# Attention logits of two heads in the two row halves of TensorE, and small float32 matmuls gathered in two banks

## The chip, the cores and the metric

The kernel runs on one core of one Trainium2 chip. The metric is the device time of one launch in microseconds (us), lower is better. TensorE does the matmuls, ScalarE and VectorE read their results out of PSUM and do the elementwise work, GpSimd does masks and reductions over partitions, and all transfers are issued from SyncE.

## The reference

One decoder layer over x of 1024 positions by 1024 channels, everything in float32. The input is normalised and projected once; the columns of the projection feed three branches:

```python
h = rms_norm(x, norm_g)
a_val, a_glu, a_gate, b_q, b_f, b_i, b_gate, c_q, c_k, c_v, c_gate, c_f, merge = split(h @ w_in)
ya = conformer_conv(a_val, a_glu, ...) * silu(a_gate)      # causal depthwise conv of width 31, LayerNorm
yb = hgrn2(b_q, b_f, b_i, ...) * silu(b_gate)              # gated linear recurrence, 8 heads of 128
yc = forgetting_attention(c_q, c_k, c_v, c_f + bias, ...) * silu(c_gate)   # 16 heads of 64
mixed = sum over branches of sigmoid(merge) * (y @ w_branch)
out = x + mixed @ w_out

# forgetting attention, per head, with q and k normalised per head:
logits = q @ k.T / 8 + F[query] - F[key]     # F: cumulative log-sigmoid of c_f
p = softmax(where(key <= query, logits, -inf));  o = p @ v

# recurrence: state = decay * state + k v^T, o = q state; here worked in chunks with levels of 2, 8, 32, 128 steps
```

## The kernel before

**Precision.** A large operand is kept as two float32r parts, high and low (high = rounded copy, low = the rest), and a product is three matmuls: high x high, high x low, low x high. The small matmuls of the recurrence, of the softmax with V, and the transposes are plain float32, which the trace shows as two records a matmul (one for a transpose).

**Staging.** `lin` is the main line: a list of projection jobs, each one weight column block of 128 against 1024 positions, in two halves of 512 and 8 x 3 matmuls each. For each c of 0 to 7 the first part of the list has eight jobs: q, k, v, gate of two attention heads (2c and 2c+1, 64 channels each, so 128 partitions), then q, forget, value, gate of recurrent head c. Everything between those jobs is done in coroutines that issue small matmuls. After that come the conv and merge-gate jobs, the branch projections and the output projection, which this change doesn't touch.

**Order.** `Sched` is a planner that runs while the program is built. It keeps an estimated time for each engine (`use`, `mm`, `act`, ...), and at each point resumes the first coroutine whose ready time has come on TensorE's clock, otherwise the next piece of `lin`. A coroutine that yields a number is ready at that time. The tile framework then orders each engine's instructions by its own timeline and sets the waits.

**Buffers.** Eight PSUM banks of 128 x 512: three rotate among the jobs of `lin`, five (`xbanks`) serve all coroutines through `bget` and `bput`. Work buffers of 1056 columns come from a pool `F` with `NF1` late and `NF2` early slots; job preludes wait until enough are free.

**Attention.** `k_done` (lines 457 to 469) scales k by its norm weight and stores it out of PSUM. For head h the tile `Khi[h]` has k's high part in both 64-row halves, `Klo[h]` the low part in one half and zeros in the other. At its end `qkprep` stores q as `Qst[h]`: high part in one half of the rows, low part in the other. So `Khi[h]` against `Qst[h]` sums high x high and high x low over 128 rows at once, and `Klo[h]` against `Qst[h]` adds low x high. `att` (line 573) walks the blocks of 256 queries from the last to the first, and for each the key blocks j of 128 up to the diagonal; for one j it takes one bank, does two matmuls for each head and evicts the two heads with ScalarE (line 604, adding the forget bias), then yields. Whole blocks have 256 queries; the last key block of each query block has 128. `soft` (line 612) masks, takes the maximum over keys by GpSimd, exponentiates, multiplies with V into `po` (line 655, each head in a 64-column half), and multiplies the folded sum `M` by ones (line 660) into the other half of the same bank.

**Recurrence.** `hgrn` (line 707) works levels of 2, 8 and 32 steps on 32-column quarters of the array, then the chunks of 128: transposes of k (line 831), state products (line 842), the chain of state updates on VectorE (line 852), and outputs (lines 867 and 869). The last four were done by halves of 512 columns with one bank each, and the planner waited `OGY` (3500 ns) or `OGZ` after each half.

Of the kernel before, what the change touches and what calls it, by code (L numbers as in the profile page):

```python
# [8 lines left out]
F32 = mybir.dt.float32  # L9
# [10 lines left out]
P = 128  # L20
# [7 lines left out]
NF2 = 8  # L28
# [171 lines left out]
def build(tc, x, norm_g, w_in, conv_w, conv_b, ln_g, ln_b, hgrn_g, f_bias, qn_g, kn_g,  # L200
# [256 lines left out]
    def k_done(st):  # L457
        def f(half, hs, ps):
            for h in range(2):
                a = slice(h * 64, h * 64 + 64)  # L460
                b = slice(64 - h * 64, 128 - h * 64)
                sc.act(Khi[h][a, hs], ps[a, :], AF.Copy, scale=gk[a])
                sc.act(Khi[h][b, hs], ps[a, :], AF.Copy, scale=gk[a])
                sc.stt(Klo[h][a, hs], ps[a, :], gk[a], Khi[h][a, hs].bitcast(F32),
                       ALU.mult, ALU.subtract)
            sc.act(st["sk"][:, hs], ps, AF.Copy)
            if half == 1:
                sc.start(qkprep(st), f"qk{st['c']}")
        return f

    def qkprep(st):
# [101 lines left out]
    def att(st):  # L573
# [6 lines left out]
        for i in (3, 2, 1, 0):  # L580
# [801 lines left out]
```

## Time and profile before

| what | value |
|---|---|
| median of 3 runs | 1957.88 us (1956.65 to 1960.06) |
| profiled execution | 1957.62 us, span of its instructions 1955.9 us |
| granted TensorE clock, mean of the span | 0.997 |
| busy, TensorE / VectorE / ScalarE / GpSimd | 1908.0 / 1275.5 / 955.5 / 196.4 us |
| DMA, mean | 72 GB/s |

The span runs from the first to the last instruction of the program on the chip; the profiled execution's own time is a little longer. Busy time of TensorE counts a matmul from its start to its modelled end, and successive matmuls overlap, so the start-to-start distance tells what one costs. Names in the rows are the program's tiles: `hT_hi`, `hT_lo` are the normalised input, `whi`, `wlo` a job's weights, `fa` and `fb` work buffers, `gt` an operand of the recurrence, `bank` a PSUM bank. A row says out<-in, then rows x columns of the array in use (128\*128 is all of it, 128\*64 a half, 128\*32 a quarter of its columns) and the moving operand.

### The profile page before, as it was taken

How to read it: one execution, taken by the hardware profiler on the slowest of the kernel's cores; microseconds unless marked ns; L12 is line 12 of the kernel's file. 1: busy time of each engine (PE TensorE's matmuls, PEld its weight loads, DVE VectorE, ACT ScalarE, POOL GpSimd, SP SyncE). 2: the span in 40 equal slices, each digit the busy share in tenths (PEclk: the TensorE clock that was granted, in tenths of full speed). 3: DMA queues.
4: the chain of work that ended last, by engine and by line, in shares of the span. 5: the costliest groups of instructions: out<-in, count | busy, mean ns of one | idle time of the engine just before them, and what ended most of it. 6: DMA issues, size and time to landing. Idle time of an engine off the chain costs nothing.

```text
span 1955.9 us, 27129 instructions
## 1 busy us (share of the span) xinstructions
PE 1908.0 (98%) x11112; PEld 1547.8 (79%) x11112; DVE 1275.5 (65%) x1689; ACT 955.5 (49%) x1524; POOL 196.4 (10%) x157
## 2 busy tenths in 40 slices
PE   5999999999999999999999999999999999999999
PEld 5787877877878778777787878888888888888888
DVE  6358575676664856757557999999996367513431
ACT  5657767757767687677776421111131234312210
POOL 4002120120211201212012100000000110000000
PEclk9999999999999999999999999999999999999999
DMA  4110111111111111111111232222245453212431
GB/s 144 42 44 23 58 40 44 44 34 44 44 45 44 33 44 55 34 44 44 44 44 33 87 108 65 75 70 71 88 160 172 162 175 110 81 54 87 129 120 53
DMA packets 173140, 141.35 MB, mean 72 GB/s; under 512 B 4917, under 2 KB 155445, under 8 KB 173016
## 3 DMA queue, kind: packets, MB, share of 16 engines
q1 hardware_dynamic: 173016, 139.62, 23.3%
q8 instruction: 87, 1.43, 0.3%
q14 instruction: 37, 0.30, 0.1%
HBM read 110.24 MB, written 29.36 MB: 71 GB/s over the span
## 4 chain that ended last, share of the span: by engine, by line
PE 78%; ACT 11%; DVE 5%; issue 3%; DMA 2%; POOL 1%; DVEq 0%; SPq 0%; ACTq 0%; POOLq 0%
PE bank L112 77%; ACT fb L125 5%; ACT L125 3%; DVE fa L129 2%; ACT khi L125 1%; DMA zdram<-fa 1%; ACT fa L125 1%; PE bank L116 1%; DMA fa<-zdram 1%; ACT gt L125 1%; ACT whi L347 1%; DVE wlo L348 1%; DVE fb L129 0%; DVE gt L129 0%; DVE sd L145 0%
## 5 line engine op out<-in xcount | busy, mean ns | idle before, releaser
L112 PE MATMUL bank<-hT_hi,whi 128*128 128x512 f32 x1792 | 709.0, 396 | 7.0 <-ACT fa L125 4.2
L112 PE MATMUL bank<-hT_lo,whi 128*128 128x512 f32 x1792 | 705.7, 394 | 0.0
L112 PE MATMUL bank<-hT_hi,wlo 128*128 128x512 f32 x1792 | 704.3, 393 | 0.9 <-DVE wlo L348 0.9
L112 PEld LDWEIGHTS bank<-hT_hi,whi 128*128 128x128 f32 x1792 | 337.7, 188 | 81.1 <-issue 5.6
L112 PEld LDWEIGHTS bank<-hT_lo,whi 128*128 128x128 f32 x1792 | 337.8, 189 | 72.8 <-issue 8.1
L112 PEld LDWEIGHTS bank<-hT_hi,wlo 128*128 128x128 f32 x1792 | 337.4, 188 | 71.5 <-issue 2.4
L347 ACT ACTIVATE whi<-wraw 128x1024 fp32r<-128x1024 f32 x137 | 145.3, 1060 | 385.0 <-PE bank L112 371.8
L348 DVE TENSOR_TENSOR wlo<-wraw,whi 128x1024 fp32r<-128x1024 f32 x135 | 170.9, 1266 | 201.9 <-ACT whi L347 200.1
L133 DVE SCALAR_TENSOR_TENSOR fa<-fa,taps,fa 128x1024 f32<-128x1024 f32 x240 | 299.8, 1295 | 0.5
L125 ACT ACTIVATE fa<-bank 128x512 f32<-128x512 f32 x191 | 111.3, 594 | 175.6 <-PE bank L112 166.5
L129 DVE TENSOR_TENSOR fa<-fa,fa 128x512 f32<-128x512 f32 (+3 forms) x158 | 131.0, 844 | 71.0 <-ACT fa L125 57.1
L112 PE MATMUL bank<-yhi,whi 128*128 128x512 f32 x384 | 148.7, 389 | 0.9 <-ACT whi L347 0.9
L112 PE MATMUL bank<-ylo,whi 128*128 128x512 f32 x384 | 149.2, 389 | 0.0
L112 PE MATMUL bank<-yhi,wlo 128*128 128x512 f32 x384 | 149.2, 389 | 0.0
L125 ACT ACTIVATE fb<-bank 128x512 f32<-128x512 f32 (+6 forms) x253 | 107.3, 435 | 85.5 <-PE bank L112 46.0
L129 DVE TENSOR_TENSOR fb<-fb,fb 128x256 f32<-128x256 f32 (+3 forms) x158 | 116.8, 754 | 37.8 <-ACT fb L125 22.9
L125 ACT ACTIVATE fb<-bank,negF,rk 128x256 f32<-128x256 f32 x244 | 113.2, 553 | 30.8 <-PE bank L112 22.6
L125 ACT ACTIVATE fb<-fb 128x1024 f32<-128x1024 f32 (+3 forms) x111 | 102.8, 954 | 22.3 <-DVE fb L129 20.9
L125 ACT ACT_TABLE_LOAD x83 | 106.5, 1283 | 8.9 <-DVE fb L129 7.5
L133 DVE SCALAR_TENSOR_TENSOR fa<-fa,bank 128x512 f32<-128x512 f32 x82 | 55.8, 682 | 65.1 <-PE bank L112 64.6
L112 PEld LDWEIGHTS bank<-yhi,whi 128*128 128x128 f32 x384 | 72.1, 188 | 16.2 <-ACT whi L347 1.3
L112 PEld LDWEIGHTS bank<-yhi,wlo 128*128 128x128 f32 x384 | 72.1, 188 | 15.1
(181 smaller groups left out, 2133.9 us busy)
## 6 DMA issues: line engine op xcount, KB each, us to landing
wraw<-in_w_in_dram SPq DMA_DIRECT2D x113, 512.0 KB, 3.8
wraw<-in_w_branch_dram SPq DMA_DIRECT2D x24, 512.0 KB, 3.7
zdram<-fa SPq DMA_DIRECT2D x16, 512.0 KB, 2.6
mdram<-fa SPq DMA_DIRECT2D x32, 256.0 KB, 2.1
fa<-mdram SPq DMA_DIRECT2D x16, 512.0 KB, 3.7
fa<-zdram SPq DMA_DIRECT2D x16, 512.0 KB, 4.4
fa<-in_x_dram SPq DMA_DIRECT2D x9, 512.0 KB, 7.0
yc<-fb SPq DMA_DIRECT2D x8, 512.0 KB, 3.6
```

What stands on the lines that cost most here:

```text
L112: self.nc.tensor.matmul(out, lhsT=lhsT, rhs=rhs, start=start, stop=stop)
L116: self.nc.tensor.transpose(out, in_, ident)
L125: return self.nc.scalar.activation(out, in_, func, **kw)
L129: self.nc.vector.tensor_tensor(out=out, in0=a, in1=b, op=op)
L133: self.nc.vector.scalar_tensor_tensor(out=out, in0=a, scalar=s, in1=b, op0=op0, op1=op1)
L347: pin(nc.scalar.activation(j.hi, j.raw, AF.Copy))
L348: pin(eng.tensor_tensor(out=j.lo, in0=j.raw, in1=j.hi.bitcast(F32), op=ALU.subtract))
```

## The change

q and k of the two heads are stored once, as high part and low part (`Qhi`, `Qlo`, `Khi`, `Klo`), each head in its own 64 partitions; the stacked copies go. The removed lines of the last two parts are left out below; they stand in the listing above. A logit product is now three matmuls a head over 64 rows, head 0 in rows 0 to 63 of the array and head 1 in rows 64 to 127, issued by turns and into two banks, one for each head. One visit does two key blocks. The space of the stacked copies becomes two more early buffers (`NF2` from 8 to 10). In `soft` the matmuls with V are moved behind the folded sum, next to those with ones. In `vprep` and `hgrn` the groups of small float32 matmuls that took one bank after another take two banks at once, with fewer yields.

```diff
--- before.py
+++ after.py
@@ -25,7 +25,7 @@
 NEG = -1e30
 FW = 1056
 NF1 = 10
-NF2 = 8
+NF2 = 10
 RES = 6
 HP = 300
 NLB = 3
@@ -275,12 +275,9 @@
     F.add(f1pool, NF1, "fa", False)
     f2pool = p1ctx.enter_context(tc.tile_pool(name="f2", bufs=1))
     F.add(f2pool, NF2, "fb", True)
-    Qst = [f2pool.tile([P, S], F32R, name=f"qst{h}") for h in range(2)]
-    Khi = [f2pool.tile([P, S], F32R, name=f"khi{h}") for h in range(2)]
-    Klo = [f2pool.tile([P, S], F32R, name=f"klo{h}") for h in range(2)]
+
+    Qhi, Qlo, Khi, Klo = (f2pool.tile([P, S], F32R, name=n) for n in ("qhi", "qlo", "khi", "klo"))
     Gt = [f2pool.tile([P, 4 * KT, 48], F32, name=f"gt{h}") for h in range(2)]
-    nc.vector.memset(Klo[0][64:128].bitcast(F32), 0.0)
-    nc.vector.memset(Klo[1][0:64].bitcast(F32), 0.0)
     ydram = {b: dram.tile([KT, P, S], F32, name=f"y{b}") for b in "bc"}
     zdram = dram.tile([KT, P, S], F32, name="zdram")
     mdram = dram.tile([KT, P, S], F32, name="mdram")
@@ -456,13 +453,8 @@
 
     def k_done(st):
         def f(half, hs, ps):
-            for h in range(2):
-                a = slice(h * 64, h * 64 + 64)
-                b = slice(64 - h * 64, 128 - h * 64)
-                sc.act(Khi[h][a, hs], ps[a, :], AF.Copy, scale=gk[a])
-                sc.act(Khi[h][b, hs], ps[a, :], AF.Copy, scale=gk[a])
-                sc.stt(Klo[h][a, hs], ps[a, :], gk[a], Khi[h][a, hs].bitcast(F32),
-                       ALU.mult, ALU.subtract)
+            sc.act(Khi[:, hs], ps, AF.Copy, scale=gk)
+            sc.stt(Klo[:, hs], ps, gk, Khi[:, hs].bitcast(F32), ALU.mult, ALU.subtract)
             sc.act(st["sk"][:, hs], ps, AF.Copy)
             if half == 1:
                 sc.start(qkprep(st), f"qk{st['c']}")
@@ -517,11 +509,8 @@
         fput(sq, y0)
         yield lambda: not busy["Q"]
         busy["Q"] = True
-        for h in range(2):
-            a = slice(h * 64, h * 64 + 64)
-            b = slice(64 - h * 64, 128 - h * 64)
-            sc.act(Qst[h][a, :], qg[a, sl], AF.Copy)
-            sc.tt(Qst[h][b, :], qg[a, sl], Qst[h][a, :].bitcast(F32), ALU.subtract)
+        sc.act(Qhi, qg[:, sl], AF.Copy)
+        sc.tt(Qlo, qg[:, sl], Qhi.bitcast(F32), ALU.subtract)
         fput(qg)
         st["q"] = st["k"] = True
         st["t"] = sc.cur.last
@@ -542,14 +531,13 @@
     def vprep(st, tag, cb):
         vT, V = st["vT"], st["V"]
         yield
+        pss = yield from bget(2)
+        for k in range(KT):
+            sc.tr(pss[k // 4][:, k % 4 * P:(k % 4 + 1) * P], vT[:, k * P:(k + 1) * P], ident)
         for half in range(2):
-            ps, = yield from bget(1)
-            for q in range(4):
-                k = half * 4 + q
-                sc.tr(ps[:, q * P:(q + 1) * P], vT[:, k * P:(k + 1) * P], ident)
-            sc.act(V[:, half * H2:(half + 1) * H2], ps, AF.Copy)
-            bput(ps)
-            yield
+            sc.act(V[:, half * H2:(half + 1) * H2], pss[half], AF.Copy)
+        bput(*pss)
+        yield
         fput(vT)
         st["v"] = True
         if cb is not None:
@@ -589,21 +577,27 @@
                     d = T[i][:, 0:768].rearrange("p (h t) -> p h t", h=2)
                     v = d[:, :, 0:256] if j == 2 * i else d[:, :, 256:384]
                 blks.append(v)
-            for j in range(2 * i + 2):
-                r = max(0, j - 2 * i)
-                n = 256 - P * r
-                ps, = yield from bget(1)
-                js = slice(j * P, (j + 1) * P)
-                qs = slice(256 * i + P * r, 256 * i + 256)
-                for h in range(2):
-                    o = ps[:, h * 256:h * 256 + n]
-                    sc.mm(o, Khi[h][:, js], Qst[h][:, qs], True, False, n * 0.42 + 6)
-                    sc.mm(o, Klo[h][:, js], Qst[h][:, qs], False, True, n * 0.42 + 6)
-                for h in range(2):
-                    hh = 2 * c + h
-                    sc.act(blks[j][:, h, :], ps[:, h * 256:h * 256 + n], AF.Identity,
-                           scale=st["rk"][:, j, h:h + 1], bias=negF[:, j, hh:hh + 1])
-                bput(ps)
+            for jp in range(i + 1):
+
+                pss = yield from bget(2)
+                js2 = []
+                for b in range(2):
+                    j = 2 * jp + b
+                    r = max(0, j - 2 * i)
+                    js2.append((j, slice(b * 256, b * 256 + 256 - P * r), slice(j * P, (j + 1) * P),
+                                slice(256 * i + P * r, 256 * i + 256)))
+                for j, o, js, qs in js2:
+                    for n, (k, q) in enumerate(((Khi, Qhi), (Khi, Qlo), (Klo, Qhi))):
+                        for h in range(2):
+                            a = slice(h * 64, h * 64 + 64)
+                            sc.mm(pss[h][:, o], k[a, js], q[a, qs], n == 0, n == 2,
+                                  (qs.stop - qs.start) * 0.21 + 6)
+                for j, o, _, _ in js2:
+                    for h in range(2):
+                        hh = 2 * c + h
+                        sc.act(blks[j][:, h, :], pss[h][:, o], AF.Identity,
+                               scale=st["rk"][:, j, h:h + 1], bias=negF[:, j, hh:hh + 1])
+                bput(*pss)
                 yield max(sc.t["pe"] + 200, sc.t["act"] - ATY)
             if i == 0:
                 busy["K"] = busy["Q"] = False
@@ -642,9 +636,8 @@
         sc.tt(blks[2 * i + 1], blks[2 * i + 1], B[:, :, P:256], ALU.subtract)
         sc.act(T[i][:, 0:768], T[i][:, 0:768], AF.Exp)
         yield 0
-        mark = sc.cur.last
         fold(ALU.add)
-        folded, sc.cur.last = sc.cur.last, mark
+        yield sc.cur.last + 500
         ts_ = slice(256 * i, 256 * i + 256)
         if not st.get("g"):
             yield lambda: st.get("g")
@@ -655,7 +648,6 @@
                 sc.mm(po[h * 64:(h + 1) * 64, P * r:256], V[:, j * P + h * 64:j * P + h * 64 + 64],
                       blks[j][:, h, :], j == 0, j == 2 * i + 1, (256 - P * r) * 0.88)
         fput(*T)
-        yield max(folded + 500, sc.cur.last)
         for h in range(2):
             sc.mm(po[h * 64:(h + 1) * 64, 256:512], ones64, M[:, h, :], True, True, 225)
         yield
@@ -778,7 +770,7 @@
             sc.tt(qn[:, :, 1:4, :], gv[:, :, 0:3, :],
                   Tv[:, :, 0:1].unsqueeze(3).broadcast_to([P, G, 3, m]), ALU.mult)
             yield mark
-            for cp in range(1 if m < 32 else 4):
+            for cp in range(1 if m < 32 else 2):
                 if m < 32:
                     ps, pv = yield from inner_level(k_in, Gx)
                     yield
@@ -796,23 +788,24 @@
                         for r in range(4):
                             a = slice(r * 32, r * 32 + 32)
                             sc.act(Sv[a, :, a], Sd[a], AF.Copy)
+                    bput(ps)
                 else:
...
+                    pss = yield from bget(2)
+                    pvs = [ps[:, 0:384].rearrange("p (c x) -> p c x", c=2) for ps in pss]
+                    for q in range(4):
+                        ch, pv = 4 * cp + q, pvs[q // 2]
                         Gc = Gx[:, 4 * ch:4 * ch + 4, :].rearrange("p c x -> p (c x)")
                         for a, o in ((0, slice(0, 96)), (32, slice(96, 160)), (64, slice(160, 192))):
...
+                            sc.mm(pv[a:a + 32, q % 2, o], k_in[:, ch * P + a:ch * P + a + 32],
+                                  Gc[:, o], True, True, 70)
+                    for n, pv in enumerate(pvs):
+                        off, ch = 0, 4 * cp + 2 * n
+                        for j in range(3):
+                            w = (3 - j) * m
+                            a = slice(32 * j, 32 * j + 32)
+                            sc.act(Sv[a, ch:ch + 2, (j + 1) * m:P], pv[a, :, off:off + w], AF.Copy)
+                            off += w
+                    bput(*pss)
                 if cp == 0:
                     sc.act(kn[:, :, 3, :], kv[:, :, 3, :], AF.Copy)
                     sc.tt(kn[:, :, 0:3, :], kv[:, :, 0:3, :], bc(Uv, 3), ALU.mult)
@@ -824,53 +817,41 @@
         KN, St, tmp = k_out, q_out, f
 
         yield
+        pss = yield from bget(2)
+        for ch in range(KT):
+            sc.tr(pss[ch // 4][:, ch % 4 * P:(ch % 4 + 1) * P], k_in[:, ch * P:(ch + 1) * P], ident)
         for hf in range(2):
...
+            sc.act(KN[:, hf * H2:(hf + 1) * H2], pss[hf], AF.Copy)
+        bput(*pss)
         yield
...
+        pss = yield from bget(2)
+        kvp = lambda ch: pss[ch // 4][:, ch % 4 * P:(ch % 4 + 1) * P]
+        for ch in range(KT - 1):
+            cs = slice(ch * P, (ch + 1) * P)
+            sc.mm(kvp(ch), KN[:, cs], V[:, cs], True, True, 222)
+        for ch in range(KT - 1):
+            ns = slice((ch + 1) * P, (ch + 2) * P)
+            if ch == 0:
+                sc.act(St[:, ns], kvp(ch), AF.Copy)
+            else:
+                sc.stt(St[:, ns], St[:, ch * P:(ch + 1) * P], T128[:, ch:ch + 1], kvp(ch),
+                       ALU.mult, ALU.add)
+        bput(*pss)
         fput(k_in)
...
+        yield sc.t["pe"] + OGY
         yield lambda: st.get("g")
...
+        pos = yield from bget(2)
+        for ch in range(KT):
+            cs = slice(ch * P, (ch + 1) * P)
+            o = pos[ch // 4][:, ch % 4 * P:(ch % 4 + 1) * P]
+            sc.mm(o, V[:, cs], Ss[:, cs], True, ch == 0, 222)
+            if ch:
+                sc.mm(o, St[:, cs], q_in[:, cs], False, True, 222)
+        for hf, po in enumerate(pos):
             hs = slice(hf * H2, (hf + 1) * H2)
...
             sc.act(KN[:, hs], po, AF.Square)
             sc.stt(tmp[:, hs], po, ghalf[:, c, :], st["gt"][:, hs], ALU.mult, ALU.mult)
...
+        bput(*pos)
         yield
         sc.use("pool", 7200)
         nc.gpsimd.partition_all_reduce(Ss[:, 0:S], KN[:, 0:S], P, RADD)
```

## Rows read from the trace of the kernel before

**Rows 1.** The page, its first line.

```profile
span 1955.9 us, 27129 instructions
```

**Rows 2.** Table by stretches: stretch, length, busy (count) per engine, clock, DMA, GB/s.

```profile
733.70:861.50 127.80, 125.42 (x881) 99.22 (x880) 82.17 (x133) 92.04 (x155) 20.09 (x15) 1.00 0.15 42
...
1117.10:1955.90 838.80, 827.47 (x3685) 688.80 (x3683) 551.39 (x532) 182.14 (x217) 17.22 (x9) 1.00 0.33 105
```

**Rows 3.** Timeline (start, length, engine, instruction, count) around four logit matmuls.

```profile
743.37 0.39 PE L112 MATMUL bank<-hT_hi,wlo 128*128 128x512 f32 x1
...
743.59 0.28 PE L112 MATMUL bank<-qst,khi 128*128 128x256 f32 x1
743.60 0.19 PEld L112 LDWEIGHTS bank<-qst,klo 128*128 128x128 f32 x1
...
744.07 0.40 PE L112 MATMUL bank<-hT_hi,whi 128*128 128x512 f32 x1
```

**Rows 4.** Timeline of TensorE, four logit matmuls of 128 queries.

```profile
781.42 0.22 PE L112 MATMUL bank<-qst,khi 128*128 128x128 f32 x1
...
781.81 0.45 PE L112 MATMUL bank<-hT_hi,wlo 128*128 128x512 f32 x1
```

**Rows 5.** Timeline of TensorE, four transposes between projection matmuls.

```profile
791.87 0.39 PE L112 MATMUL bank<-hT_hi,whi 128*128 128x512 f32 x1
792.10 0.60 PE L116 MATMUL bank<-ident,fa 128*128 128x128 f32 x4
792.45 0.48 PE L112 MATMUL bank<-hT_lo,whi 128*128 128x512 f32 x1
```

**Rows 6.** Timeline of TensorE, probabilities times V between projection matmuls.

```profile
794.83 0.39 PE L112 MATMUL bank<-hT_hi,whi 128*128 128x512 f32 x1
795.15 1.08 PE L112 MATMUL bank<-fb,fb 128*64 128x256 f32 x8
796.17 0.50 PE L112 MATMUL bank<-hT_lo,whi 128*128 128x512 f32 x1
796.50 0.40 PE L112 MATMUL bank<-hT_hi,wlo 128*128 128x512 f32 x1
```

**Rows 7.** Timeline of TensorE, a run of the recurrence with attention inside.

```profile
801.56 0.37 PE L112 MATMUL bank<-gt,fa 128*32 128x48 f32 x14
801.87 0.65 PE L112 MATMUL bank<-fb,ones 128*64 128x256 f32 x4
802.45 0.70 PE L112 MATMUL bank<-gt,fa 128*32 128x48 f32 x42
803.08 1.08 PE L112 MATMUL bank<-fa,fb 128*64 128x256 f32 x8
804.09 0.29 PE L112 MATMUL bank<-gt,fa 128*32 128x48 f32 x8
804.31 0.50 PE L112 MATMUL bank<-hT_hi,wlo 128*128 128x512 f32 x1
```

**Rows 8.** Timeline of TensorE; in brackets the idle time before a row.

```profile
827.48 0.89 PE L112 MATMUL bank<-gt,fa 128*32 128x48 f32 x64 [0.81 <-ACT gt L125]
828.30 0.50 PE L112 MATMUL bank<-hT_hi,whi 128*128 128x512 f32 x1
...
833.65 0.50 PE L112 MATMUL bank<-hT_hi,whi 128*128 128x512 f32 x1 [0.29 <-ACT fb L125]
...
857.63 0.49 PE L112 MATMUL bank<-fa,fb 128*128 128x128 f32 x2 [0.25 <-DVE fb L133]
```

**Rows 9.** Groups of ScalarE, 733.7 to 861.5: count, busy us, mean ns, idle before.

```profile
L125 ACT ACTIVATE fb<-bank,negF,rk 128x256 f32<-128x256 f32 x26 | 12.7, 571 | 3.7 <-PE bank L112 2.5 <-issue 1.2
...
L125 ACT ACTIVATE khi<-bank,gk 64x512 fp32r<-64x512 f32 x8 | 5.5, 685 | 0.1
...
L125 ACT ACTIVATE qst<-fb 64x1024 fp32r<-64x1024 f32 x2 | 2.1, 1053 | 0.0
```

**Rows 10.** Timeline of TensorE after the eighth period.

```profile
1133.10 0.80 PE L112 MATMUL bank<-hT_hi,whi 128*128 128x512 f32 x1 [4.20 <-ACT fa L125]
```

More of the change, by code (lines that the diff above doesn't have):

```diff
@@ L798, in hgrn @@
                             sc.act(Sv[a, :, a], Sd[a], AF.Copy)
+                    bput(ps)
                 else:
-                    ps, = yield from bget(1)
-                    pv = ps[:, 0:384].rearrange("p (c x) -> p c x", c=2)
-                    for q in range(2):
-                        ch = 2 * cp + q
+                    pss = yield from bget(2)
+                    pvs = [ps[:, 0:384].rearrange("p (c x) -> p c x", c=2) for ps in pss]
+                    for q in range(4):
+                        ch, pv = 4 * cp + q, pvs[q // 2]
                         Gc = Gx[:, 4 * ch:4 * ch + 4, :].rearrange("p c x -> p (c x)")
                         for a, o in ((0, slice(0, 96)), (32, slice(96, 160)), (64, slice(160, 192))):
-                            sc.mm(pv[a:a + 32, q, o], k_in[:, ch * P + a:ch * P + a + 32], Gc[:, o],
-                                  True, True, 70)
-                    off = 0
-                    for j in range(3):
-                        w = (3 - j) * m
-                        a = slice(32 * j, 32 * j + 32)
-                        sc.act(Sv[a, 2 * cp:2 * cp + 2, (j + 1) * m:P], pv[a, :, off:off + w],
-                               AF.Copy)
-                        off += w
-                bput(ps)
+                            sc.mm(pv[a:a + 32, q % 2, o], k_in[:, ch * P + a:ch * P + a + 32],
[8 more added lines that the diff above has]
+                    bput(*pss)
                 if cp == 0:
@@ L826, in hgrn @@
         yield
+        pss = yield from bget(2)
+        for ch in range(KT):
+            sc.tr(pss[ch // 4][:, ch % 4 * P:(ch % 4 + 1) * P], k_in[:, ch * P:(ch + 1) * P], ident)
         for hf in range(2):
-            ps, = yield from bget(1)
-            for q in range(4):
-                ch = 4 * hf + q
-                sc.tr(ps[:, q * P:(q + 1) * P], k_in[:, ch * P:(ch + 1) * P], ident)
-            sc.act(KN[:, hf * H2:(hf + 1) * H2], ps, AF.Copy)
-            bput(ps)
-            yield sc.t["pe"] + HGY
@@ L835, in hgrn @@
-        yield
-        for hf in range(2):
-            ps, = yield from bget(1)
-            for q in range(4):
-                ch = 4 * hf + q
-                if ch < 7:
-                    cs = slice(ch * P, (ch + 1) * P)
-                    sc.mm(ps[:, q * P:(q + 1) * P], KN[:, cs], V[:, cs], True, True, 222)
-            for q in range(4):
-                ch = 4 * hf + q
-                if ch == 7:
-                    break
-                kvp = ps[:, q * P:(q + 1) * P]
-                ns = slice((ch + 1) * P, (ch + 2) * P)
-                if ch == 0:
-                    sc.act(St[:, ns], kvp, AF.Copy)
-                else:
-                    sc.stt(St[:, ns], St[:, ch * P:(ch + 1) * P], T128[:, ch:ch + 1], kvp,
-                           ALU.mult, ALU.add)
-            bput(ps)
-            yield sc.t["pe"] + OGY
+            sc.act(KN[:, hf * H2:(hf + 1) * H2], pss[hf], AF.Copy)
@@ L856, in hgrn @@
+        bput(*pss)
         fput(k_in)
-        yield
+        yield sc.t["pe"] + OGY
         yield lambda: st.get("g")
-        pst = []
-        for hf in range(2):
-            hs = slice(hf * H2, (hf + 1) * H2)
-            po, = yield from bget(1)
-            for q in range(4):
-                ch = 4 * hf + q
-                cs = slice(ch * P, (ch + 1) * P)
-                o = po[:, q * P:(q + 1) * P]
-                sc.mm(o, V[:, cs], Ss[:, cs], True, ch == 0, 222)
-                if ch:
-                    sc.mm(o, St[:, cs], q_in[:, cs], False, True, 222)
+        pos = yield from bget(2)
@@ L873, in hgrn @@
-            yield sc.t["pe"] + OGZ
+        bput(*pos)
         yield
```

1 line of the change is left out of this document (removed).

## Prediction

> **What bounds the kernel now.** I read the page first, then the table by stretches, then TensorE's timeline. The span is 1955.9 us [rows 1] and the profiled execution took 1957.6 us, 1.7 us around it; the median of three runs is 1957.88, so a sum made against 1957.6 can be read against either. The change touches only the part with the recurrence and the attention. There the work repeats eight times, once for each pair of attention heads with one recurrent head. One such period is 127.8 us; TensorE is busy in 125.4 us of it at a granted clock of 1.00, VectorE in 82, ScalarE in 92 [rows 2]. The rest of the program, 839 us, has TensorE busy in all but 11 us and no line of it changes [rows 2]. So a period is TensorE's list of matmuls, and the change is priced by what it adds to and takes from that list, times 8.
>
> **What one matmul costs.** Start to start is what counts, since matmuls overlap. A projection matmul (512 columns) takes 0.23 us. A logit matmul of 256 columns takes 0.12: the first of four starts at 743.59, 0.22 after the projection before it, and the next projection follows at 744.07, 0.48 later [rows 3]. Four of 128 columns take 0.39, and the projection behind them lasts 0.45 instead of 0.39: 0.45 together [rows 4]. Four transposes start an ordinary 0.23 after a projection and take 0.35, plus 0.09 by which the next row is longer: 0.11 each [rows 5]. All these use the whole array (128 rows by 128 columns), and passing from one such kind to another costs nothing.
>
> Matmuls on part of the array are different. Eight records of probabilities times V, on 64-column halves, stand between projections that start at 794.83 and 796.50 [rows 6]. Eight take 1.02 [rows 6] and four 0.58 [rows 7], so two are worth 0.22. Of the 1.67 us, 2 x 0.23 and 4 x 0.22 are work, and 0.33 to 0.35 is neither: the entry takes 0.32 instead of 0.23, the first pair is slow, and the first projection after it has 0.33. **A visit to another division of the array costs 0.35 us.** The same inside a run on 32-column quarters: from 801.56 to 804.31 stand 64 quarter records, four half records and eight [rows 7]. 64 quarter records take 0.82 (827.48 to 828.30) [rows 8], the halves 0.44 and 0.88; of 2.75 us 0.61 is left for two interruptions, 0.30 each.
>
> The Trainium skill has this rule (TensorEngine Tiling (Array Packing), Tiling Modes): changing the tiling mode, unlike changing the tile, drains TensorE. The trace agrees, at 0.35 us a visit; a sum without it would be that of the first rival below.
>
> **The logits.** Now 16 key blocks of 256 queries and 4 of 128 take four full-array matmuls each in a period, q stacked as high and low part in 128 rows. Afterwards a visit does two blocks in three steps each (high-high, high-low, low-high), and a step is two matmuls, one head in each 64-row half. That is ten visits a period, six with two full blocks and four on the diagonal with a full and a half one. No row of before has row halves, so their price is bounded. From below: the two heads of a step run together, a step costs 0.12 (0.11 at 128 columns, as the transposes), and entering is free, as among the full-array kinds [rows 3, 5]. From above: each matmul takes its own 0.12 and a visit its switch. The nearest rows are the column tiles. Do those overlap? If the records on halves ran one by one at 0.11 for 256 columns, one of 48 columns would take 0.021 and 64 of them 1.3 us; they take 0.82 [rows 8], weight loads included, so several quarters run at once. I take overlap for row halves too, and a switch of 0.40: the 0.35 of column halves, plus 0.05 because a row half loads 128 weight columns before its first step and not 64 (a load with its matmul paces at 0.11 for 128 [rows 5]).
>
> Full visit: 6 x 0.12 + 0.40 = 1.12 against 2 x 0.48 = 0.96, +0.16. Diagonal: 3 x 0.12 + 3 x 0.11 + 0.40 = 1.09 against 0.48 + 0.45 = 0.93, +0.16. Ten visits are +1.6, eight periods **+13 us**: the shorter stream is eaten by the switches. Lower bound: 0.40 less a visit, -0.24 x 80 = -19. Upper bound: 12 x 0.12 + 0.40 = 1.84 against 0.96, and 6 x 0.12 + 6 x 0.11 + 0.40 = 1.78 against 0.93; 6 x 0.88 + 4 x 0.85 = 8.7 a period, +69.
>
> **Softmax.** Now the matmuls with V go out as soon as the exponentials are there, the column sums with ones only after the folded sum. In a period of the timeline that makes eight visits from the full array and two interruptions of quarter runs ([rows 6] is one of the first kind, [rows 7] has both of the second). The change waits for the folded sum and 500 ns of the planner's time, then issues both together: four visits. Gone are 4 x 0.35 + 2 x 0.30 = 2.0 a period, **-16 us**; the matmuls themselves stay. If V's matmuls are still split, half of that, -8. Behind the new wait in its own coroutine stand only these matmuls; if VectorE's fold is later on the chip than in the plan, TensorE stops, and the next projection stands behind. The score buffers are held for the length of the fold; the two added buffers stand against that.
>
> **k and q.** Storing k takes eight ScalarE copies of 64 rows (685 ns) and becomes two; q's two copies (1053 ns) become one [rows 9]. ScalarE loses 6 x 0.68 + 1.05 = 5.1 us a period, VectorE half of its subtractions there. Neither bounds the period, so only TensorE's waits count. The gaps before 827.48 (0.81, for a ScalarE copy into the recurrence's operand) and 833.65 (0.29) [rows 8] stand among the eight copies. Recovering 0.8 of these 1.1 is my choice, between 0 and 1.1. The wait on the recurrence's state chain (0.25 before 857.63 [rows 8]) will have all its products ahead of it and one planner wait behind: 0.2. Together 1.0, **-8 us**, between 0 and -11.
>
> **Gathered matmuls.** The transposes of V and K, the state products and the outputs use the whole array, so fewer groups of them save nothing by themselves; the 32-step level is on quarters, but its four groups already stand in one run. I take zero, covered by projections between. Uncovered, TensorE waits for one bank copy (0.57 by the nearest row [rows 9]) at each of four gathered groups a period, +18. After the eighth period TensorE stops 4.20 us for a chain that begins at the last recurrence [rows 10]; its state products no longer wait for the planner twice: **-2 us**, between 0 and -4.
>
> Sum: 1957.6 + 13 - 16 - 8 - 2 = 1944.6, **1945 us**.
>
> **Rivals.** *Row halves switch free*: the logits are -19 in place of +13, 1957.6 - 19 - 26 = 1913. For it: the full-array kinds switch free [rows 3 to 5]. Against: every partial-array visit of the trace pays [rows 6, 7].
>
> *Row halves don't overlap*, the one that ends slower: matmuls or their weight loads go one by one, 1957.6 + 69 - 26 = 2001. Against: column tiles overlap, loads too [rows 8]. For: no row has row tiles, and the load of 128 weight columns at 0.11 already fills a step of 0.12, so that any hitch between the two heads' loads shows in full. It decides from 0.15 us a step: my gain of 13 us over 480 steps is 0.027 on top of 0.12. The Trainium skill (TensorE: Matmul & The Clock Gate, Part 3) lets a weight load run under matmuls only where their row groups differ; by that a step's loads would wait for the step before, 0.23 a step, about this rival. On the whole array the trace disagrees: the load at 743.60 begins with the matmul at 743.59 on the same rows [rows 3].
>
> *Two banks per visit*: five banks serve all the small work; a visit's two are emptied by four ScalarE evictions of 0.57 us [rows 9], 2.3 us, and the recurrence now asks for two as well. If TensorE stood 0.25 us at each of the 80 visits, +20, the time is 1965. Against: TensorE idles only 2.4 us of a period [rows 2], and none of its gaps there is before a logit.
>
> **How the numbers follow.** My forecast has 0.55, with its own range 1930 to 1957 (a switch of 0.30 there; softmax half as good and few waits recovered here). Free switch 0.10, no overlap 0.17, banks 0.18. About 0.2% (3.9 us) is what a measurement of this kernel can tell from no change. Faster by more: 0.50 of the forecast, all of the free switch and 0.02 of the banks, 0.62. Within: 0.05 of the forecast and 0.05 of the banks, 0.10. Slower: 0.17 and 0.11, 0.28. The range 1918 to 1990 leaves out most of the free switch (0.07) and of no overlap (0.13).
>
> **What would show it.** Right: logit matmuls in pairs a few ns apart, 0.12 from pair to pair, 0.3 us or more on entry; four V visits a period with the ones in the same run; the gaps at the quarter run and at the bank gone; a period of about 126.3 us. Wrong: a projection an ordinary 0.23 after row halves; pair partners 0.1 apart; V's matmuls still cut by projections; new gaps before logits, released by ScalarE. What most likely misleads me is the price of a row-half visit, then the order into which the planner now puts everything.

## The result: slower by 17.7 us, and the profile after

The changed kernel takes 1975.66 us (median of 4 runs, 1973.79 to 1976.01) against 1957.94 of the kernel before: a ratio of 1.0088, 95% interval [1.0075, 1.01]. The forecast was 1945, faster. The time lies in the stated range of 1918 to 1990; the sign is wrong.

First the page's first line and three stretches of 130 us, to be held against [rows 1, 2]. The columns are those of [rows 2].

```profile
span 1974.3 us, 27620 instructions
```

```profile
478.00:608.00 130.00, 126.89 (x930) 100.54 (x931) 87.26 (x137) 85.08 (x148) 26.98 (x16) 0.96 0.13 37
608.00:738.00 130.00, 128.77 (x912) 98.71 (x910) 76.51 (x122) 91.10 (x149) 13.73 (x14) 1.00 0.16 45
738.00:868.00 130.00, 125.90 (x931) 100.12 (x932) 88.11 (x137) 85.89 (x149) 27.00 (x16) 0.97 0.13 37
```

The periods now go by pairs: every second one has a granted clock below 1.00, which no period of before had. TensorE's timeline shows why, in four of the eight periods (280.26, 539.71, 800.71 and 1060.45):

```profile
739.28 0.94 PE L112 MATMUL bank<-fa,fa 128*128 128x128 f32 x6 [1.38 <-DVE fb L133]
...
797.35 0.54 PE L112 MATMUL bank<-gt,fb 128*32 128x48 f32 x30
800.71 1.08 PE L112 MATMUL bank<-fb,fb 128*64 128x256 f32 x8 [2.81 <-ACT fb L125]
801.72 0.46 PE L112 MATMUL bank<-gt,fb 128*32 128x48 f32 x22
802.11 0.54 PE L112 MATMUL bank<-qhi,khi 64*128 64x256 f32 x1
...
804.13 0.63 PE L112 MATMUL bank<-hT_lo,whi 128*128 128x512 f32 x1
804.55 0.63 PE L112 MATMUL bank<-hT_hi,wlo 128*128 128x512 f32 x1
...
808.82 0.48 PE L112 MATMUL bank<-hT_hi,whi 128*128 128x512 f32 x1
809.14 0.40 PE L112 MATMUL bank<-hT_lo,whi 128*128 128x512 f32 x1
```

In the middle of a run on quarters stand eight matmuls with V whose exponentials ScalarE had not finished. TensorE stops for 2.81 us, and the other 22 records of the run start only behind them, at 801.72, without a wait of their own. ScalarE was late because it had itself waited for VectorE:

```profile
799.60 1.06 ACT L125 ACTIVATE fb<-fb 128x1024 f32<-128x1024 f32 x1 [1.77 <-DVE fb L129]
```

From 802.2 to 809.0 TensorE's clock is granted at half, 1.2 GHz: projection matmuls start 0.43 us apart instead of 0.23. The stop of 1.38 us is of another kind. Its six records are state products, whose operands VectorE doesn't write; VectorE was still reading the bank that they go into:

```profile
738.54 1.29 DVE L133 SCALAR_TENSOR_TENSOR fb<-bank,fb 128x512 f32<-128x512 f32 x2 [5.30 <-ACT fb L125]
```

The logits, which no row of before could show:

```profile
753.39 0.39 PE L112 MATMUL bank<-hT_hi,wlo 128*128 128x512 f32 x1
753.71 0.38 PE L112 MATMUL bank<-qhi,khi 64*128 64x256 f32 x2
753.93 0.28 PE L112 MATMUL bank<-qlo,khi 64*128 64x256 f32 x2
...
754.40 0.28 PE L112 MATMUL bank<-qhi,klo 64*128 64x256 f32 x2
754.61 0.50 PE L112 MATMUL bank<-hT_hi,whi 128*128 128x512 f32 x1
754.95 0.40 PE L112 MATMUL bank<-hT_lo,whi 128*128 128x512 f32 x1
```

A row x2 is one step, both heads together (here their records start 3 ns apart). Steps follow at 0.12; entry takes 0.32 and the first projection behind 0.34, each 0.23 among ordinary neighbours. From projection to projection it is 1.56, less 2 x 0.23: **1.11 us a visit**. The visit on the diagonal (766.60 to 768.09) is 1.03. Not every visit has both heads. The order that the tile framework made sets some apart, such as this one; by its shapes, its other head stands in the rows x1 from 802.11 above.

```profile
796.57 0.33 PE L112 MATMUL bank<-qhi,khi 64*128 64x256 f32 x1
```

In 69 of the change's 480 steps the two heads don't start together. A head alone saves nothing: its six steps take 0.78 us here, to the row at 797.35.

To compare orders, each span is split in three below, from all TensorE records after the first 60 us: *idle*, the idle times over 0.06 us in front of records; *half clock*, half the start-to-start time while the granted clock was 0.5; and *list*, the span less both, which is what TensorE's matmuls would take in this order without stops at full clock.

| | span | idle | half clock | list |
|---|---|---|---|---|
| before | 1955.9 | 22.5 | 1.6 | 1931.8 |
| after | 1974.3 | 24.6 | 15.3 | 1934.4 |

Of 18.4 us, 13.7 are half clock, 2.1 idle, 2.6 list.

### The profile page after: what moved, and what is told of

Same layout as the page of the kernel before. It is cut to its first block, busy times and chain, and to the rows that moved or that the text cites. A ratio compares the mean times of both kernels' runs of the same rounds, so it can differ in the third digit from the quotient of the medians.

```text
span 1974.3 us, 27620 instructions
## 1 busy us (share of the span) xinstructions
PE 1925.5 (98%) x11432; PEld 1548.9 (78%) x11432; DVE 1267.5 (64%) x1663; ACT 922.9 (47%) x1474; POOL 200.9 (10%) x157
## 5 line engine op out<-in xcount | busy, mean ns | idle before, releaser
L129 DVE TENSOR_TENSOR fa<-fa,fa 128x512 f32<-128x512 f32 (+3 forms) x236 | 186.5, 806 | 62.9 <-ACT fa L125 30.9
L125 ACT ACTIVATE fb<-bank 128x512 f32<-128x512 f32 (+6 forms) x302 | 135.3, 462 | 97.4 <-PE bank L112 69.1
L129 DVE TENSOR_TENSOR fb<-fb,fb 128x512 f32<-128x512 f32 (+4 forms) x159 | 118.6, 764 | 69.9 <-ACT fb L125 48.7
L125 ACT ACTIVATE fa<-bank 128x512 f32<-128x512 f32 (+1 forms) x142 | 82.3, 584 | 168.0 <-PE bank L112 151.0
L125 ACT ACTIVATE fa<-fa 128x1024 f32<-128x1024 f32 (+3 forms) x87 | 71.8, 830 | 76.0 <-DVE fa L129 38.0
L125 ACT ACTIVATE fb<-fb 128x1024 f32<-128x1024 f32 (+4 forms) x91 | 82.8, 915 | 37.5 <-DVE fb L129 33.8
L125 ACT ACTIVATE fb<-bank,negF,rk 128x256 f32<-128x256 f32 (+1 forms) x160 | 74.9, 553 | 30.4 <-PE bank L112 25.9
```

The source lines that it names most:

```text
L125: return self.nc.scalar.activation(out, in_, func, **kw)
L129: self.nc.vector.tensor_tensor(out=out, in0=a, in1=b, op=op)
```

## Experiments

The theories in the expectations: A, TensorE's order and its stops, with the half clock behind them; B, row halves are the whole loss; C, visits of two banks; D, the operations of the edits themselves.

### One part at a time

`e1_logits` is before with the row halves, the storage of q and k and two more buffers; `e2_soft` with the softmax edit; `e3_gather` with the gathered matmuls; `e4_no_soft` is the change without the softmax edit:

```diff
+        mark = sc.cur.last
         fold(ALU.add)
-        yield sc.cur.last + 500
+        folded, sc.cur.last = sc.cur.last, mark
...
+        yield max(folded + 500, sc.cur.last)
```

> Only the logits in row halves, with q and k stored once and the two added buffers; softmax and gathered groups as before. Theory A (the row halves cost what was forecast, the loss comes from stalls that the new order of the three edits together makes): ten visits at +0.16 us in eight periods are +13, ScalarE's relief takes back up to 8, so 1963 to 1971 us, and no stretch at half clock within the periods. Theory B (the row halves are the whole loss): 1975 us or more, with the same stops before the matmuls with V. Theory C (waits for two banks in the recurrence): as A.

> Only the move of the matmuls with V behind the folded sum. As forecast: 16 us less, 1942 us, four visits a period on column halves. Theory A: the matmuls with V are still cut into pieces by the order that the tile framework makes, 1950 to 1960 us, and the count of changes of the array's division from full to column halves stays near 63 in all periods together. Theory B: no effect, 1956 to 1960. Theory C: as A.

> Only the gathered groups of small float32 matmuls in the value transposes and in the recurrence, two banks at once. Theory A: no tile change is saved and no work, 1954 to 1961 us. Theory B: the same. Theory C (the state products now wait until both banks are free, 1.4 us at half of the periods, and half clock follows from the idle time): 6 to 15 us more, 1964 to 1973.

> The change without the move in softmax: row halves and gathered groups. Theory A, if the move makes the stops of 2.8 us before the matmuls with V: these and the half clock behind them are gone, which is 11 + 14 us of the change's time, so 1951 to 1965. If the stops belong to the row halves' order (theory B): 1972 to 1978 as the whole change. Theory C: the 1.4 us waits before the state products stay, five of them or more.

| | median us | ratio, 95% | idle | half clock | list |
|---|---|---|---|---|---|
| e1_logits | 1979.91 | 1.0113 [1.0096, 1.0129] | 24.8 | 12.5 | 1940.5 |
| e2_soft | 1965.62 | 1.0038 [1.0023, 1.0053] | 34.2 | 7.8 | 1920.3 |
| e3_gather | 1999.31 | 1.0213 [1.0197, 1.0228] | 64.9 | 15.8 | 1916.1 |
| e4_no_soft | 1982.78 | 1.0129 [1.0114, 1.0144] | 27.6 | 9.9 | 1944.5 |

e1 falls where theory B had it and not A; e2, e3 and e4 lie outside every range given. Each part alone is slower than before, and they don't add: 22 + 8 + 42 against 18 together. Two parts *shorten* the list, by 12 and 16 us, and lose it again in stops. The worst stop of `e3_gather` is of the kind seen above:

```profile
845.24 1.12 PE L112 MATMUL bank<-fb,fb 128*64 128x256 f32 x4 [3.50 <-ACT fb L125]
```

### The order alone

`e7_order_only` is before with the same instructions; only the planner's guess for a logit matmul is half as large again.

```diff
-                    sc.mm(o, Khi[h][:, js], Qst[h][:, qs], True, False, n * 0.42 + 6)
-                    sc.mm(o, Klo[h][:, js], Qst[h][:, qs], False, True, n * 0.42 + 6)
+                    sc.mm(o, Khi[h][:, js], Qst[h][:, qs], True, False, n * 0.63 + 6)
+                    sc.mm(o, Klo[h][:, js], Qst[h][:, qs], False, True, n * 0.63 + 6)
```

> The kernel before with one number of the planner changed: it counts a logit matmul with 0.63 ns a column and not 0.42. The instructions are the same, only their order differs. Theory A (most of what these edits cost is the new order: TensorE issues in order and stops where another engine is later than the plan assumed): slower than before by 5 us or more, with stops of over 1 us in the periods that before doesn't have. Theory D (the edits' own operations cost it): within 3 us of before, 1955 to 1961.

1972.96 us, 1.0071 [1.0056, 1.0086]: idle 40.7, half clock 1.6, list 1928.2. The same work in another order costs 14 us, nearly the loss of the change. The list is 3.6 us shorter; the loss is in stops such as these of one period:

```profile
711.85 1.66 PE L112 MATMUL bank<-gt,fa 128*32 128x96 f32 x48 [1.29 <-ACT gt L125]
723.77 0.66 PE L116 MATMUL bank<-ident,fb 128*128 128x128 f32 x4 [1.67 <-ACT fb L125]
737.87 0.94 PE L112 MATMUL bank<-fa,fa 128*128 128x128 f32 x6 [1.77 <-DVE fb L133]
```

Theory D misses, and an order alone can cost this much. That it did so in the change is not shown by this run; e15 below decides it.

### Forcing the four visits of V and ones

In `e8_ones_first` (on the change) and `e9_before_ones_first` (on before with the softmax edit) the ones go first and V's matmuls, pinned in program order, follow at once:

```diff
+        for h in range(2):
+            sc.mm(po[h * 64:(h + 1) * 64, 256:512], ones64, M[:, h, :], True, True, 225)
+        js = [2 * i, 2 * i + 1] + list(range(2 * i))
-        for j in range(2 * i + 2):
+        for j in js:
...
+                tc.keep_in_program_order(
+                    sc.mm(po[h * 64:(h + 1) * 64, P * r:256], ...))
```

> The whole change, and in softmax the matmuls with ones go first and those with V are pinned behind them, beginning with the key blocks exponentiated last, so that a visit to the column halves can't be cut by an operand that is late. Theory A: the four stops of 2.8 us and the half clock behind them are gone and visits to column halves fall from 78 to 32 to 40, so 25 us for the stops and 13 to 16 us for the visits less than the changed kernel, 1934 to 1952, if no new stop of another kind comes in its place. Theory D: 1970 to 1978.

> The kernel before with the softmax edit alone in the form with the ones first and V pinned behind. The forecast's step of -16 us is tested: four visits a period to column halves, 32 to 40 in all. Theory A: the periods shorten by 1.5 to 2 us each, 12 to 16 in all; what of it reaches the end depends on the stops at the passage to the branch projections, 1940 to 1960. Theory D: as the softmax edit alone, 1963 to 1967.

1969.2 us, 1.0052 [1.0037, 1.0067], and 1991.26, 1.0163 [1.0146, 1.018]. Entries into column halves fall from 77 (the change) and 58 (e2) in the program to 32 and 30, and the list to 1920.7 and 1906.2, 14 us shorter in both: 0.30 and 0.50 us for an entry saved, on both sides of the forecast's 0.35. But idle rises to 34.3 and 56.2 and the half clock to 14.6 and 26.5. Pinned work waits for its last operand, and all of TensorE behind it. Both times lie outside the ranges of A and of D.

### The planner's waits

`e10_wait2500` gives the new wait of `soft` 2500 ns in place of 500. `e11_before_of_wait` is `e9_before_ones_first` with the same. The others change `MARGIN`, the time by which the planner lets a coroutine rest that yields no time of its own: 2500 in place of 1500, in `e12_before_of_margin` on e11, in `e13_after_of_margin` on e8 with the wait of 2500, in `e14_after_margin` on the change with nothing else. `e15_margin_periods` is e14 with 1500 again once the last period's buffers are free, and `e16_before_margin_periods` is before with these margins, the control.

```diff
-    MARGIN = 1500.0
+    MARGIN = 2500.0
...
         yield lambda: prog["c"] == KT and prog["b"] == KT and len(F.early) == NF2
+        sc.MARGIN = 1500.0
```

> The whole change with the planner's wait behind the folded sum at 2500 ns and not 500. The operations are the same. Theory A: the matmuls with V stand 2 us later in TensorE's order, so the stops of 2.8 us go or shrink below 1 us, and the half clock with them: 1945 to 1962, unless the new order brings other stops. Theory D: 1970 to 1980.

> The kernel before with the softmax edit alone, ones first, V pinned, and 2500 ns of planner time behind the folded sum in place of 500. Theory A (TensorE's list gets shorter by the visits saved, and the time is decided by the stops that the order makes): the stops of 1.8 us before the ones go, the list without stops stays some 20 us shorter than before's, the time comes to 1945 to 1975 by what other stops are left. Theory D (the operations decide, the order is a detail): within 5 us of the same edit with 500 ns, 1986 to 1996.

> As the last one, and the planner's margin before it resumes any coroutine at 2500 ns and not 1500. Theory A: everything that TensorE is given was finished longer ago by the plan, so fewer and shorter stops in the periods, 1940 to 1970; the chain at the passage to the branch projections gets longer by some us. Theory D: 1986 to 1996.

> The whole change with ones first, V pinned, 2500 ns behind the folded sum, margin 2500. Theory A: few stops and no half clock in the periods, about the changed kernel's list less 13 to 16 us of visits, 1935 to 1960. Theory D: 1967 to 1978.

> The changed kernel with nothing but the margin at 2500 ns in place of 1500: same operations. Theory A: another order, other stops, a time that differs from 1975.7 by 5 us or more, downwards if the longer margin does what it is for: 1945 to 1970. Theory D: 1972 to 1979.

> The whole change with the planner's margin at 2500 ns in the eight periods and back at 1500 ns from the passage to the branch projections on, so that the 10.9 us stop at 1647 us, which the longer margin made in the later part, should go. Theory A (the change's operations are worth about nothing, its loss is stops and half clock): 1967 less 10 to 14, 1953 to 1958, level with the kernel before or up to 5 us faster. Theory D (the operations cost some 15 us): 1966 to 1975.

> The control to that run: the kernel before with the same two margins, same operations as before. Theory A: another order brings other stops, so a time at least 3 us from 1957; 1960 to 1980, as the order of before was the best of several. If instead the longer margin is good for any version: 1945 to 1955, and then the change's operations are worth less than the margin. Theory D: 1955 to 1960.

| | median us | ratio, 95% | idle | half clock | list |
|---|---|---|---|---|---|
| e10_wait2500 | 1968.16 | 1.0046 [1.0031, 1.0061] | 31.1 | 6.9 | 1928.1 |
| e11_before_of_wait | 2037.39 | 1.0408 [1.0393, 1.0424] | 99.0 | 29.5 | 1905.1 |
| e12_before_of_margin | 1985.65 | 1.0147 [1.013, 1.0163] | 64.2 | 9.4 | 1908.7 |
| e13_after_of_margin | 1986.34 | 1.0146 [1.0131, 1.0161] | 48.6 | 18.3 | 1916.2 |
| e14_after_margin | 1968.51 | 1.0054 [1.0039, 1.0069] | 26.7 | 4.4 | 1936.1 |
| e15_margin_periods | 1958.31 | 1.0001 [0.9992, 1.0009] | 16.3 | 1.7 | 1937.4 |
| e16_before_margin_periods | 1956.58 | 0.9994 [0.9985, 1.0003] | 25.1 | 5.3 | 1924.2 |

A longer wait doesn't mean fewer stops: the one number of e10 and of e11 moved the time by -7.5 and by +46 us against the kernels they were made from. Of the seven, A's range holds for e14 alone (e15 lies 0.3 us above its range), D's for the control e16; e10 to e13 lie outside both. With `MARGIN` alone the stops of 2.8 us leave the periods, and the half clock but for 3.4 us in the first (e14); a stop of 1.5 us in each period remains. But the part behind them, which the change never touched, got another order and this stop:

```profile
1647.58 0.79 PE L112 MATMUL bank<-hT_hi,whi 128*128 128x512 f32 x1 [10.91 <-DVE fa L133]
```

With the old margin there (e15) **the change is level with before**: its instructions are the same as in the kernel that lost 17.7 us. That takes theory D down (1966 to 1975), and B as the whole cause, for the row halves are still in it. The control e16 is level with before as well, in time and not in its parts: its list is 7.6 us shorter, its idle 2.6 and its half clock 3.7 us longer.

### Two more of the order

On e15, `e17_v_pinned` pins V's matmuls in a row with the ones behind. `e18_head_major` is the change with the loop over heads outside that over the three products, meant to take the overlap away.

```diff
-                    for n, (k, q) in enumerate(((Khi, Qhi), (Khi, Qlo), (Klo, Qhi))):
-                        for h in range(2):
+                    for h in range(2):
+                        for n, (k, q) in enumerate(((Khi, Qhi), (Khi, Qlo), (Klo, Qhi))):
```

> As the whole change with the two margins, and in softmax the matmuls with V begin with the key blocks exponentiated last and are pinned in a row, the ones pinned behind them: each softmax is one visit to the column halves. Theory A: some 32 to 36 such visits, TensorE's list 13 to 16 us shorter than without the pins; 1940 to 1960 if no stop over 2 us comes with it, up to 1975 if stops before the ones (the folded sum late on VectorE) do. Theory D: 1966 to 1975.

> The changed kernel with one head's three matmuls of a key block issued before the other head's, not by turns; nothing else. If neighbours in opposite row halves overlap and those in the same half follow each other, a visit has nine steps in place of six, +0.34 us at each of 80 visits: 1975.7 + 27 = 1998 to 2006. If the row halves do not overlap (the forecast's second rival), no change by this: 1972 to 1980.

`e17_v_pinned` took 1959.92, 1.0011 [1.0002, 1.0019]: list 4.7 us under that of e15, idle 3.3 and half clock 5.2 over. That lies in A's range, but not for its reason: the entries into column halves fell from 80 to 56 and not to some 32, and the list was to fall by 13 to 16. `e18_head_major` took 1973.52, 1.008 [1.0066, 1.0094], and I had expected far more. It tested nothing, though the time lies in the range for no overlap: the framework, which orders instructions by its own timeline, put most of the heads by turns again (400 steps of 480 as pairs).

```profile
746.63 0.39 PE L112 MATMUL bank<-qhi,khi 64*128 64x256 f32 x2
746.85 0.29 PE L112 MATMUL bank<-qlo,khi 64*128 64x256 f32 x2
```

A kernel with all heads apart was not tried; what a head alone costs stands in the next part.

### Which part pays, in an order with few stops

The margins of e15 and e16 allow a comparison of parts. `e20_soft_margin` is e16 with the softmax edit. `e19_no_logits_margin` adds the gathered matmuls; from it to e15 only the logits, the storage of q and k and the two buffers are missing.

```diff
-NF2 = 10
+NF2 = 8
...
-    Qhi, Qlo, Khi, Klo = (f2pool.tile([P, S], F32R, name=n) for n in ("qhi", "qlo", "khi", "klo"))
+    Qst = [f2pool.tile([P, S], F32R, name=f"qst{h}") for h in range(2)]
...
```

> The change without its logit part (stacked q and k, eight early buffers), planned with the margins of the run before (2500 ns in the periods, 1500 behind them). Theory A, order and stops on top of TensorE's list: the softmax and gather parts shorten the list (their single runs had 1920 and 1916 us of it against 1932) and the logit part alone lengthens it (1940), so the list is 1905 to 1915; with the stops of an order of that kind, 20 to 45 us, the run takes 1930 to 1955 and is the fastest so far. Theory B, row halves are the whole loss of the change: at or under 1958, for the row halves are gone. Theory C, visits of two banks are the loss: 1975 or more, since the gathered groups stay.

> Before with the softmax edit alone, planned with the same margins (2500 ns in the periods, 1500 behind them). Theory A: the edit alone gave a list of 1920 us and 34 us of stops, 12 of them at the loads of the branch projections; an order without these stops gives 1943 to 1953, one with them 1958 to 1966. Theories B and C: neither row halves nor two banks are in it, so it is level with before or faster, 1940 to 1960.

| added to the one above | median us | ratio, 95% | idle | half clock | list |
|---|---|---|---|---|---|
| e16 (before) | 1956.58 | 0.9994 [0.9985, 1.0003] | 25.1 | 5.3 | 1924.2 |
| softmax: e20 | 1947.28 | 0.9947 [0.9933, 0.996] | 24.6 | 2.9 | 1918.1 |
| gathers: e19 | **1931.82** | **0.9863 [0.9849, 0.9876]** | 14.3 | 0.0 | 1915.8 |
| logits, q and k, buffers: e15 | 1958.31 | 1.0001 [0.9992, 1.0009] | 16.3 | 1.7 | 1937.4 |

Theory A gave e19 1930 to 1955 and e20 1943 to 1953; both came there, though e19's list is 0.8 us above what A gave and its stops below. B allowed e19 as well, and here the row halves are indeed the one part that costs; C, with 1975 or more, falls. **e19 is faster than both kernels.** In these margins, each with the order that it got, the softmax edit comes to -9 us, the gathers to -15 (2 of them list, the rest stops and half clock) and the row halves with what belongs to them to +26. One period of e19 and one of e15, in the table by stretches:

```profile
592.55:717.07 124.52, 123.34 (x881) 100.16 (x881) 84.22 (x133) 92.56 (x155) 21.38 (x15) 1.00 0.15 43
```

```profile
557.59:685.11 127.52, 126.02 (x920) 98.86 (x920) 78.18 (x130) 87.51 (x147) 21.55 (x15) 1.00 0.15 42
```

Summed start to start by the kind of matmul, idle apart, the 3.0 us between them are logits +0.84 (9.40 to 10.24), the same 384 projections +1.77 (89.77 to 91.54; each first one behind a visit is longer), V and ones +0.31, idle +0.32, the rest -0.2. Logits and projections together are 2.6 a period, 21 us in eight: nearly all of the 22 by which the list grows. The rest of the partial-array work is cut up hardly more: the column halves are entered 10 times a period in e15 and 8 times in e19. The logits stand in 11 visits instead of the ten planned, and four of the 11 have one head alone. Two of them:

```profile
657.61 0.38 PE L112 MATMUL bank<-qhi,khi 64*128 64x256 f32 x1
658.44 0.65 PE L112 MATMUL bank<-fa,ones 128*64 128x256 f32 x4
659.02 0.38 PE L112 MATMUL bank<-qhi,khi 64*128 64x256 f32 x1
```

The first takes 0.83 us for its six steps, as both heads together do (0.83 from 633.93). Two visits a period more, at 1.03 each, are 16 us in eight periods: an estimate, but most of the 22. So the larger part of what row halves cost here is again the order, and no run kept all heads together.

## Why the forecast was wrong, step by step

The forecast's span was 1942.9 (1944.6 less the 1.7 around it), the measured one 31.4 us longer. In the split used here it had list 1931.8 + 13 - 16 = 1928.8, idle 22.5 - 10 = 12.5 and half clock 1.6. Measured: list +5.6 against that, idle +12.1, half clock +13.7. In the margins of e15 and e16 the same sum fails elsewhere: from e16 to e15 idle falls by 8.8, near the forecast's 10, and the list rises by 13.2 where the forecast had -3.

- **Matmul prices: right.** A row-half visit was put at 1.12 and 1.09 us and takes 1.11 and 1.03; where they stand together the two heads do overlap, and the rival without overlap (2001) falls with the rows at 753.71. But I took it that they always stand together. In the change 69 of 480 steps don't (117 in e1, 149 in e4, 100 in e15), which at 0.12 a step is some 8 us in the change, an estimate. The free switch falls too: entry 0.32, re-entry 0.34. The Trainium skill (TensorEngine Tiling (Array Packing), Tiling Modes) says that a change of mode drains TensorE; the trace agrees for row halves as it did for column halves.
- **Logits, +13: right for a visit with both heads, too small for the order.** By those prices ten visits are 6 x 0.15 + 4 x 0.10 = 1.3 a period, +10. The part as a whole lengthened the list by 9 us alone (e1) and by 22 between e19 and e15, with the runs of V and ones there. Some 16 of these 22 are heads set apart, by the estimate above; what the storage of q and k and the buffers hold was not separated.
- **Softmax, -16: too much.** The list falls by 11.5 (e2) and by 10 (e4 to the change); with the margins of e16 by 6. The four visits a period never came, 77 entries into column halves in the change against 80 before: the framework still cuts V from the ones, in the change too.

```profile
810.16 1.08 PE L112 MATMUL bank<-fb,fb 128*64 128x256 f32 x8
811.08 0.82 PE L112 MATMUL bank<-fa,fb 128*64 128x256 f32 x8
811.83 0.50 PE L112 MATMUL bank<-hT_hi,wlo 128*128 128x512 f32 x1
...
813.65 0.65 PE L112 MATMUL bank<-fa,ones 128*64 128x256 f32 x4
```

- **k and q, -8 of waits: this is the step that failed.** The old gaps did go, but I let the recovered time stand as if the order stayed. The new one put other waits in (1.38 and 2.81 us above, once in two periods each), and idle went up by 2.1 instead of down by 10. I had written that TensorE stops if the fold is late (the stop of 2.81 us is for the exponentials, not for the fold) and named the order as what would mislead me, but gave it no price in the sum and no rival of its own.
- **The half clock, 13.7 us, was no term at all.** The row for it was there in [rows 10]: a stop of 4.20 us in front of a projection lasting 0.80 instead of 0.39. The Trainium skill (TensorE: Matmul & The Clock Gate, HAM oscillation) warns of idle gaps that drop the clock. Its case waits for DMA; the trace agrees for the wait for ScalarE before 800.71, with the clock at 0.5 from 802.2 on.
- **Gathers, 0 and -2 behind the last period: open in sign.** The 4.20 us stop is gone. The stop of 1.38 us, 5.5 us over the four, stands before gathered state products, which I had taken as covered. Else the gathers are +42 us alone (e3, by stops) and -15 on top of the softmax edit in good margins (e20 to e19: idle -10, half clock -3, list -2), neither of them the forecast's zero.
- **Two banks:** in the change six stops stand before logits (0.19 at 655.66, for ScalarE), 1.1 us in all against the rival's 20, so the rival (1965) is not what happened. The 1.38 us are a wait for a bank, but taking two at once isn't needed for it: e7, with one bank a group, has the same stop of 1.77 at 737.87.

Shown: the order carries the loss of 17.7 us. e7 makes one of 14 us without a new instruction, and e15 removes that of the change without one. Not shown: that the change gains in any order; e15 is no faster than its control e16. Open: why the planner and the framework reach a bad order in one setting and a good one in another. Each was read from the trace afterwards, none was foreseen, and e8 to e13 show that my guesses of a better one were mostly bad.

## What to carry to other kernels

Where the program's order is made by a planner, every edit is also a throw of its order: time an edit in several settings of one knob, and the kernel before in the same settings, before calling the edit good or bad (here softmax and gathers were +8 and +42 us in one setting and -9 and -15 in the other, the gathers there on top of the softmax edit). Split each time into matmul list, stops and half clock. The list moves least with the order, but it moves: by up to 9 us among kernels with the same instructions (before, e7 and e16; the change, e10, e14 and e15), idle by up to 18. Half-array matmuls that halve the streamed columns win only if the visits are long against their switches: 1.11 us here where the full array needed 0.96. And read in the trace whether the two halves run together; issuing them by turns doesn't keep them so.

## What the runs showed of the hardware

- The price of a stop is not its length. Behind the stops of 2.8 us in the change the granted clock was 0.5 for 6.8 to 10.2 us, 3.4 to 5.1 us of lost time each (15.3 over the four); behind those of 1.4 us it stayed at 1.00. Nor does the length decide whether the clock falls: in e17 the same pair of stops, 1.34 and 0.55 us, stands in seven periods, and in four of them 3.4 us at 0.5 followed. What else decides was not found.
- Two matmuls on 64-row halves with their own weights start 3 ns apart (at 753.71) and pass 256 columns each in 0.12 us a pair, weight loads included; the diagonal's steps of 128 columns take 0.06 to 0.11. One head alone takes the same 0.12 (796.57 on).
